# All pairs of the second MLP matrix by seven products, with sums kept in PSUM over the slices and two of the seven added by VectorE

## Chip, cores and metric

One NeuronCore of a Trainium2 chip runs the whole kernel. The metric is the device time of one execution in microseconds. Engines are called as in the profile: PE (TensorE) multiplies, PEld loads its stationary operand, DVE (VectorE) and ACT (ScalarE) do elementwise work, POOL (GpSimd) next to nothing here, and SP issues the DMAs.

## What is computed

A decoder trunk of two layers over 256 tokens with a model dimension of 2048, all in float32. Layer 0 mixes with a gated short convolution, layer 1 with latent attention (16 heads); each layer then has an MLP, and each sub-layer ends in a post-norm `x <- LN(alpha*x + f(x))`. The change lies in the two MLPs:

```python
def sq_relu_mlp(x, w1, w2):                       # x (256, 2048), w1 (2048, 8192), w2 (8192, 2048)
    return jnp.square(jax.nn.relu(x @ w1)) @ w2

h = layer_norm(ALPHA * h + mix, ln_g[layer, 0], ln_b[layer, 0])
h = layer_norm(ALPHA * h + sq_relu_mlp(h, mlp_w1[layer], mlp_w2[layer]), ln_g[layer, 1], ln_b[layer, 1])
```

## The kernel before, in words

**Precision.** Every float32 operand is split into a high part that PE multiplies in one pass and a low rest: ACT makes the high part by a cast (`split`, L127), DVE the rest by a subtraction (L128). A product then takes three matmuls: high x high, high x low, low x high (`dot`, L300, L302, L303).

**Weights.** They stream from DRAM in loads of 128 x 1024 (512 KB) on SP's queue into a ring of `RAW` = 5 raw buffers, are split, and stand in a ring of `WA` = 8 pairs of high and low buffers. `take` (L183) hands the next weights to the consumer and, before that, writes out the preparing steps up to `LOOK` = 5 steps ahead, so the order in which DVE and ACT get their work follows the order of consumption; a scheduler then moves single instructions within it.

**An MLP** (`mlp`, L575) goes over the hidden dimension in eight slices, q = 0 to 7, of eight chunks of 128 each. In the up half of a slice, `products` (L288) makes eight sums over 16 blocks of w1, each a matmul of 512 columns and one of 256 (L215, L219); `hidden` (L713) takes each out of PSUM, applies relu and square, and splits it. In the down half the slice is multiplied with its rows of w2 and added to the output, which is kept in SBUF as `acc`, 256 tokens x 2048 columns.

**The six inner slices** (`FAST`, q = 1 to 6, in both layers twelve) form the down products two by two: a pair of hidden chunks and the two halves of the tokens make a 2 x 2 block matrix, the pair's weights for two blocks of 512 columns another, and seven products in place of eight give the four results (`FACTORS`, L339). The price are sums of the blocks: of the inputs by `form` (L703), four DVE operations and a split for each pair; of the weights in `prepare` (L141), three DVE subtractions (L162, L166, L169) and two further splits for each pair. There are two groups g of two column blocks and four pairs j in each. `MIXED` = "sssp" says that in the first group only three pairs go that way ("s"); the fourth ("p") is done plainly with eight products, from two plain loads of w2. So a slice has three fast pairs and a plain one, then four fast pairs.

**Sums.** The seven running sums of a group are not folded into the output at each slice. Four of them ("1", "5", "7", "6": `OWN`) have a place of their own in the tile `sums`, three have the place of an output block. Before a group's matmuls ACT copies a sum from its place into a PSUM bank (`resumed`, L608), the matmuls add onto it, and afterwards ACT copies it back (`put_back`, L615) or DVE adds a freshly begun sum onto the place (`keep`, L618). All seven leave PSUM after each group. `fold` (L669) combines them in the last slice. Of the eight banks, four serve the up sums, and they change places with the others from slice to slice.

**Order around it.** The residual `xres` (16 chunks of 128 x 256) stays in SBUF throughout. In layer 0, `begin` subtracts a mean from its chunks in the last slice; in layer 1, `extra` turns it by 32 transposes on PE and adds it to `acc`, a quarter in each of the slices 1 to 4.

Of the kernel before, what the change touches and what calls it, by code (L numbers as in the profile page):

```python
# [16 lines left out]
P = 128  # L17
W = 256 + 2
T = 256
# [14 lines left out]
RAW, WA = 5, 8  # L34
# [3 lines left out]
MIXED = "sssp"  # L38
EVEN = (QC - 1, "22")
# [7 lines left out]
WO_G = 3  # L47
BEHIND = (2, 2, 2, 3, 2, 2, 3)
# [5 lines left out]
def trunk(ctx: ExitStack, tc: tile.TileContext, xT, vecs, lead, w_first, w_in, w_out, w_kv, w_q, w_uk, w_uv,  # L54
# [12 lines left out]
    xres = act.tile([P, NC, T], F32, tag="xres", name="xres")  # L67
    for tag, columns in (("c", 4096), ("a2", 4128), ("a1", 4128), ("b", 8256)):
        act.tile([P, columns], F32, tag=tag, name=f"at_{tag}")
# [7 lines left out]

    stream = []
# [20 lines left out]
    stream += halves(w_o) + mlp_stream(1)  # L99

# [40 lines left out]
    def prepare(i):  # L141
# [7 lines left out]
        r1, r2 = (load_raw(f"{i}_{j}", src) for j, src in enumerate(stream[i]))  # L149
        out = []  # L150

        def finished(r, name):
# [3 lines left out]

        b22, (b21, b12) = r1[:, BW:], (r2[:, :BW], r2[:, BW:])
# [12 lines left out]
        f = state["fast"].tile([P, 2, BW], F32R, tag="t4", name=f"t4_{i}", bufs=2)  # L170
        split(f[:, 0, :], f[:, 1, :], t4)
        b1, t13, b2 = ([[v.rearrange("p b c -> p (b c)")[:, o:o + BW] for v in w] for o in (0, BW)] for w in out)
        ready[i] = {"11": b1[0], "22": b1[1], "21": b2[0], "T2": b2[1], "T1": t13[0], "T3": t13[1],
                    "T4": [f[:, 0, :], f[:, 1, :]]}
# [168 lines left out]
    def fast_products(ps, x, forms, j, fresh, ready, onto=()):  # L343

        b, = take(1)
        a = {"11": held(x[2 * j], 0), "12": held(x[2 * j + 1], 0), "22": held(x[2 * j + 1], 1)}
        for i in range(4):
            a[f"S{i + 1}"] = [forms[:, j, o, i * P:(i + 1) * P] for o in range(2)]
        for p, l, r in FACTORS:
            dot(ps[p], b[r], a[l], p in fresh, p in ready, onto=p in onto)  # L350

# [40 lines left out]
    class Norm:  # L392
# [10 lines left out]
        def prepare(self, m, bank=None):  # L403

            d = xres[:, m, :]
# [11 lines left out]
        def count(self, m):  # L417
            d = xres[:, m, :]
# [21 lines left out]
        def wide(self, m):  # L440
            d, x, g = xres[:, m, :], self.xd[m], self.gain(m)[0]
# [31 lines left out]
        def normal(self, m, dst=None):  # L473

            g, b = self.gain(m)
            d = xres[:, m, :]
# [22 lines left out]
    def add(ps, m):  # L499
        d = xres[:, m, :]  # L500
        nc.vector.tensor_tensor(d, d, ps[:, :T], ALU.add)

    def summed(ln, pss, add, m0=0):

        for m, ps in enumerate(pss, m0):
            add(ps, m)
# [40 lines left out]
    ln = Norm(0, ALPHA)  # L547
    for m in range(NC):
# [19 lines left out]
        if m >= NC // 2:  # L568
            for k in range(2 * m - NC, 2 * m - NC + 2):
                ln.prepare(k)  # L570
    nc.sync.dma_start(id_t, ident)
    ln.widen("a1", "a2")
    summed(ln, chain(products(1, z), lagged(NC - 1, z)), residual)

    def mlp(idx, ln, blocks, fast, begin=None, extra=None, last=False):  # L575
# [25 lines left out]
        sums = fast.tile([P, 4, 2, BW], F32, name=f"sums{idx}")  # L601

        def place(p, g):

            return sums[:, OWN.index(p), g, :] if p in OWN else \
                block(*{"2": (2 * g, 0), "3": (2 * g + 1, 0), "4": (2 * g, 1), "22": (2 * g + 1, 1)}[p])

        def resumed(p, g, name, bank):  # L608

            ps = psum(name, bank)  # L610
            if q != FAST[0] or p not in OWN:
# [3 lines left out]
        def put_back(p, g, ps):  # L615
            nc.scalar.copy(place(p, g), ps)

        def keep(p, g, ps):  # L618

            at = place(p, g)  # L620
            if q == FAST[0] and p in OWN:
# [4 lines left out]
        def resume(busy, free, ps, m):  # L626

            b2, b3, b4, b6 = free
            b1, b5, b7, b22 = busy
# [558 lines left out]
```

## Time and profile before

| what | us |
|---|---|
| three timed runs | 1996.66, 1998.59, 1999.63; median 1998.59 |
| span of the profiled execution (the page gives no other time for it) | 1994.9 |
| PE busy | 1987.7 |
| PEld busy | 1737.2 |
| DVE busy | 1709.4 |
| ACT busy | 1354.9 |

The granted TensorE clock is 1.000. HBM is read at 381.78 MB in all, 192 GB/s over the span. How to read it: matmuls are pipelined, so the duration of one (some 390 ns for 512 columns) is longer than the distance between two starts; busy time is the union over an engine's instructions. The inner slices of layer 0 begin near 454, 537, 620, 703, 787 and 870 us, those of layer 1 near 1396, 1480, 1564, 1648, 1732 and 1815 us; the up half takes a little over half of each.

### The profile page before, as it was taken

The page shows a single profiled execution, that of the slowest core. Times are in us where ns is not written, and L with a number is a line of the kernel's source. Part 1 is how long each engine was busy: PE and PEld are TensorE (multiplying, and loading weights), DVE is VectorE, ACT ScalarE, POOL GpSimd, SP SyncE. Part 2 cuts the span into 40 slices and gives each one's busy share as a digit, 9 for nine tenths or more (in the row PEclk, how much of TensorE's full clock was granted, in tenths as well). Part 3 has the DMA queues.
Part 4 walks back from the last instruction along what each step waited for, and adds up shares of the span by engine and source line. Part 5 has one row for each costly group of instructions (what it writes and reads, how often), then busy time and mean ns, then how long its engine had stood idle before and what let it go on. Part 6 is the DMA issues. An engine that isn't in the chain of part 4 may idle for free.

```text
span 1994.9 us, 30180 instructions
## 1 busy us (share of the span) xinstructions
PE 1987.7 (100%) x11110; PEld 1737.2 (87%) x11110; DVE 1709.4 (86%) x2555; ACT 1354.9 (68%) x2154; POOL 2.3 (0%) x21
## 2 busy tenths in 40 slices
PE   9999999999999999999999999999999999999998
PEld 8888888988888888888889998898888888888886
DVE  8667667797999989989978988777899999999985
ACT  6444445586778778777756755558677787887772
POOL 0000000000000000000000000000000000000000
PEclk9999999999999999999999999999999999999999
DMA  8666666565657466574855543656464656656483
GB/s 318 205 191 187 190 190 190 179 193 157 212 170 251 148 216 221 177 243 147 281 171 159 170 140 123 201 180 195 146 233 155 232 161 220 222 178 233 150 269 130
DMA packets 106853, 385.85 MB, mean 193 GB/s; under 512 B 11857, under 2 KB 12625, under 8 KB 106449
## 3 DMA queue, kind: packets, MB, share of 16 engines
q1 hardware_dynamic: 106560, 383.79, 59.5%
q8 instruction: 87, 1.43, 0.3%
q14 instruction: 62, 0.50, 0.1%
q10 hardware_dynamic: 144, 0.13, 0.0%
HBM read 381.78 MB, written 2.10 MB: 192 GB/s over the span
## 4 chain that ended last, share of the span: by engine, by line
PE 98%; DVE 1%; ACT 1%; issue 0%; DVEq 0%; ACTq 0%
PE ps_u L215 20%; PE ps_l L215 13%; PE ps_u L219 10%; PE ps_l L219 7%; PE ps_f L300 4%; PE ps_f L303 4%; PE ps_f L302 4%; PE ps_r L303 4%; PE ps_r L302 4%; PE ps_r L300 4%; PE ps_d L300 2%; PE ps_d L302 2%; PE ps_d L303 2%; PE ps_w L249 2%; PE ps_w L248 2%; PE ps_w L247 2%
## 5 line engine op out<-in xcount | busy, mean ns | idle before, releaser
L128 DVE TENSOR_TENSOR lo<-raw,hi 128x1024 fp32r<-128x1024 f32 x710 | 861.8, 1220 | 190.6 <-ACT hi L127 119.9
L127 ACT CAST hi<-raw 128x1024 fp32r<-128x1024 f32 x710 | 741.8, 1051 | 247.4 <-PE ps_l L215 98.1
L215 PE MATMUL ps_u<-xhl,hi 128*128 128x512 f32 x1792 | 621.7, 392 | 0.0
L219 PE MATMUL ps_u<-xhl,lo 128*128 128x256 f32 x1792 | 498.2, 279 | 0.0
L215 PEld LDWEIGHTS ps_u<-xhl,hi 128*128 128x128 f32 x1792 | 334.5, 187 | 73.6 <-ACT acc L595 0.2
L219 PEld LDWEIGHTS ps_u<-xhl,lo 128*128 128x128 f32 x1792 | 338.1, 189 | 1.8
L215 PE MATMUL ps_l<-xhl_a,hi 128*128 128x512 f32 x704 | 244.1, 393 | 0.0
L219 PE MATMUL ps_l<-xhl_a,lo 128*128 128x256 f32 x704 | 195.4, 279 | 0.0
L215 PEld LDWEIGHTS ps_l<-xhl_a,hi 128*128 128x128 f32 x704 | 132.1, 188 | 29.9
L219 PEld LDWEIGHTS ps_l<-xhl_a,lo 128*128 128x128 f32 x704 | 131.9, 188 | 0.2
L127 ACT CAST hi_t<-raw_t 128x1024 fp32r<-128x1024 f32 x84 | 88.5, 1054 | 45.8 <-DVE raw_t L162 41.4
L162 DVE TENSOR_TENSOR raw_t<-raw,raw 128x1024 f32<-128x1024 f32 x84 | 102.3, 1218 | 1.8 <-DMA raw<-in_w2f_dram 1.5
L128 DVE TENSOR_TENSOR lo_t<-raw_t,hi_t 128x1024 fp32r<-128x1024 f32 x84 | 102.4, 1219 | 0.2
L718 ACT ACTIVATE fp<-fp 128x256 f32<-128x256 f32 x96 | 40.0, 416 | 63.2 <-DVE fp L356 62.6
L215 PE MATMUL ps_l<-z,hi 128*128 128x512 f32 x240 | 82.4, 391 | 0.0
L300 PE MATMUL ps_d<-hi,h 128*128 128x512 f32 x192 | 75.0, 391 | 0.0
L302 PE MATMUL ps_d<-lo,h 128*128 128x512 f32 x192 | 75.0, 390 | 0.0
L303 PE MATMUL ps_d<-hi,h 128*128 128x512 f32 x192 | 74.8, 389 | 0.0
L249 PE MATMUL ps_w<-xd,hi 128*128 128x258 f32 x256 | 72.7, 284 | 0.0
L248 PE MATMUL ps_w<-xd,lo 128*128 128x258 f32 x256 | 72.3, 282 | 0.0
L247 PE MATMUL ps_w<-xd,hi 128*128 128x258 f32 x256 | 72.3, 282 | 0.0
L215 PE MATMUL ps_l<-oT,hi 128*128 128x512 f32 x208 | 71.3, 391 | 0.0
(296 smaller groups left out, 3963.7 us busy)
## 6 DMA issues: line engine op xcount, KB each, us to landing
raw<-in_w_dram SPq DMA_DIRECT2D x344, 512.0 KB, 4.5
raw<-in_w2f_dram SPq DMA_DIRECT2D x168, 512.0 KB, 3.9
raw<-in_w_in_dram SPq DMA_DIRECT2D x88, 512.0 KB, 4.2
raw<-in_w_out_dram SPq DMA_DIRECT2D x32, 512.0 KB, 3.7
raw<-in_w_o_dram SPq DMA_DIRECT2D x32, 512.0 KB, 4.2
raw<-in_w_kv_dram SPq DMA_DIRECT2D x10, 512.0 KB, 3.7
raw<-in_w_q_dram SPq DMA_DIRECT2D x8, 512.0 KB, 4.0
raw<-in_w_uk_dram SPq DMA_DIRECT2D x8, 512.0 KB, 3.9
```

The source lines that it names most:

```text
L127: nc.scalar.copy(hi, src)
L128: nc.vector.tensor_tensor(lo, src, hi.bitcast(F32), ALU.subtract)
L162: nc.vector.tensor_tensor(t.rearrange(two, a=2), b12.unsqueeze(1).to_broadcast([P, 2, BW]), r1.rearrange(two, a=2), ALU.subtract)
L215: nc.tensor.matmul(ps, w[blk // 8][0][:, blk % 8, :], x, start=first, stop=False)
L219: nc.tensor.matmul(ps[:, :T], w[blk // 8][1][:, blk % 8, :], x[:, :T], start=False, stop=last)
L247: nc.tensor.matmul(ps[:, :W], hi, x[k][:, :W], start=k == 0, stop=False)
L248: nc.tensor.matmul(ps[:, :W], lo, x[k][:, :W], start=False, stop=False)
L249: nc.tensor.matmul(ps[:, :W], hi, x[k][:, W:], start=False, stop=k == NC - 1)
L300: nc.tensor.matmul(ps, x[0], w[0], start=first, stop=False, skip_group_check=onto)
L302: nc.tensor.matmul(ps[:, at], x[0], w[1][:, at], start=False, stop=False, skip_group_check=onto)
L303: nc.tensor.matmul(ps, x[1], w[0], start=False, stop=last, skip_group_check=onto)
L718: nc.scalar.activation(f, f, AF.Relu)
```

## The change

- Every pair of both groups is a fast one; `MIXED` and the plain pairs go.
- The two groups change their order from slice to slice (`groups`): the second group of a slice is the first of the next. Four of its sums ("3", "1", "5", "7") stay in their PSUM banks over the next up half; "2", "6" and "4" are copied out and, in the middle of the next up half, in again (`first_sums`).
- At the change of group inside a slice the last pair of the first group is followed product by product: as soon as a sum's last matmul is issued, it is taken out (`turn`) and its bank takes the next sum of the second group. Sums "3" and "1" (`FRESH`) begin there from nothing, and DVE adds them onto their place when they leave; the other five are copied in and out by ACT.
- The input factors of a pair lie in one tile of seven blocks, made by three DVE operations and one split (`form`); relu and square run over the two chunks of a pair at once.
- The residual is written to DRAM (`parked`) in slice 1 of layer 0, the tile `sums` takes its place in SBUF, and in slice 7 it is loaded again (`xback`). `begin` moves from the last slice to slice 1. In layer 1 all of `extra` moves to slice 1.
- The rings grow: `RAW` from 5 to 7, `WA` from 8 to 9.
- A way of preparing weight factors ahead and storing them in DRAM (`EARLY`) is written but empty here; its code is left out below.

```diff
-RAW, WA = 5, 8
+RAW, WA = 7, 9
-MIXED = "sssp"
-EVEN = (QC - 1, "22")
+EARLY = {}
+FRESH = ("3","1")
...
+    def groups(q):
+        return (1, 0) if (q - FAST[0]) % 2 == 0 else (0, 1)
...
-            for j, kind in enumerate(MIXED):
-                out += [(w2f[l, q, 1, j, 0], w2f[l, q, 1, j, 1])] if kind == "s" else \
-                    halves(w2[l, q, 2, j]) + halves(w2[l, q, 3, j])
-            out += [(w2f[l, q, 0, j, 0], w2f[l, q, 0, j, 1]) for j in range(QC // 2)]
+            for i, g in enumerate(groups(q)):
+                for j in range(QC // 2):
+                    out.append((w2f[l, q, g, j, 0], w2f[l, q, g, j, 1]) + made.get((l, q, i, j), ()))
...
+        def first_sums(ps, banks, m):
+            g = groups(q)[0]
+            for p in {3: ("3", "1", "5", "7") if q == FAST[0] else (), 4: "2", 5: "6", 6: "4"}.get(m, ()):
+                banks.setdefault(p, busy[m % 4])
+                ps[p] = begun_sum(p, g, f"ps_r{p}", banks[p])
+
+        def new_sum(p):
+            return p in FRESH or (q == FAST[0] and p in OWN)
+
+        def begun_sum(p, g, name, bank):
             ps = psum(name, bank)
-            if q != FAST[0] or p not in OWN:
+            if not new_sum(p):
                 nc.scalar.copy(ps, place(p, g))
             return ps
...
+        def keep(p, g, ps, since):
             at = place(p, g)
-            if q == FAST[0] and p in OWN:
+            if p not in FRESH or (since == FAST[0] and p in OWN):
                 nc.scalar.copy(at, ps)
             else:
                 nc.vector.tensor_tensor(at, at, ps, ALU.add)
...
+            def begin_next(p, bank):
+                after[p], place_of[p] = begun_sum(p, second, f"ps_f{p}", bank), bank
+
+            def turn(p):
+                keep(p, first, ps[p], max(q - 1, FAST[0]) if p in order[:4] else q)
+                i = order.index(p) + 1
+                if i < len(order):
+                    begin_next(order[i], banks[p])
+
+            def end(p):
+                if p not in stay:
+                    keep(p, second, after[p], q)
+
+            held_on = set(order[:4]) if q > FAST[0] else set()
+            for j in range(n):
+                if j == n - 1:
+                    begin_next(order[0], spare)
+                fast_products(ps, h, j, new - held_on if j == 0 else (), ps if j == n - 1 else (),
+                              set(ps) - (new - held_on), turn if j == n - 1 else None)
+            for j in range(n):
+                fast_products(after, h, j, new if j == 0 else (), after if j == n - 1 else (),
+                              set(order) - new, end if j == n - 1 else None)
...
+            def form(j, u):
+                a21, a11, a12, s1, s2, s4 = (u[:, i * P:(i + 1) * P] for i in (0, 1, 3, 4, 6, 7))
+                two = u.rearrange("p (i c) -> p i c", c=P)
+                nc.vector.tensor_tensor(s1, a21, u[:, 2 * P:3 * P], ALU.add)
+                nc.vector.tensor_tensor(two[:, 5:7, :], two[:, 0:5:4, :], a11.unsqueeze(1).to_broadcast([P, 2, P]),
+                                        ALU.subtract)
                 nc.vector.tensor_tensor(s4, a12, s2, ALU.subtract)
-                split(forms[:, j, 0, :], forms[:, j, 1, :], sf.rearrange("p i c -> p (i c)"))
+                f = factors[j // 2][:, j % 2]
+                split(f[:, 0, :], f[:, 1, :], u[:, P:])
...
-                    if extra and m == 0 and q <= NB:
+                    if extra and q == FAST[0] and m < NB:
                         for t in range(2):
-                            extra(block, q - 1, t, busy[2 + t])
+                            extra(block, m, t, busy[2 + t])
+                    if begin and q == FAST[0]:
+                        begin(range(max(2 * m, 1), 2 * m + 2))
+                        nc.sync.dma_start(parked[:, 2 * m:2 * m + 2, :], held_x[0][:, 2 * m:2 * m + 2, :])
+                    if q == FAST[0] and m == QC - 1:
+                        sums = act.tile([P, 4, 2, BW], F32, tag="xres", name=f"sums{idx}")
...
+                if begin and q == NQ - 1:
+                    held_x[0] = act.tile([P, NC, T], F32, tag="xres", name="xback")
+                    for k in range(0, NC, 4):
+                        nc.sync.dma_start(held_x[0][:, k:k + 4, :], parked[:, k:k + 4, :])
```

More of the change, by code (lines that the diff above doesn't have):

```diff
@@ L47 @@
 WO_G = 3
+MAKE_FROM = 6
 BEHIND = (2, 2, 2, 3, 2, 2, 3)
@@ L169, in prepare @@
         nc.vector.tensor_tensor(t4, b21, b12, ALU.subtract)
[L170 to L174, printed above, removed]
+        ready[i] = {**named((("11", "22"), ("T1", "T3"), ("21", "T2"))), "T4": fourth(t4)}
         yield
```

193 lines of the change are left out of this document (102 added, 91 removed).

## The prediction

> **What bounds the kernel now.** Read the page first: the busy shares, then the chain that ended last.
>
> ```profile
> span 1994.9 us, 30180 instructions
> ...
> PE 1987.7 (100%) x11110; PEld 1737.2 (87%) x11110; DVE 1709.4 (86%) x2555; ACT 1354.9 (68%) x2154; POOL 2.3 (0%) x21
> ...
> PE 98%; DVE 1%; ACT 1%; issue 0%; DVEq 0%; ACTq 0%
> ```
>
> TensorE is the chain: whoever takes matmuls away shortens the kernel, as long as the engines that feed it keep up. VectorE's mean of 86% hides stages. So the second view is the windows, one for each slice of the hidden dimension that is multiplied with the seven-product scheme (here three inner ones of the first layer, two of the second, one down half, and the ends).
>
> ```profile
> 536.98:620.21 83.23, 83.23 (x429) 71.28 (x429) 78.12 (x102) 66.78 (x104) 0.00 (x0) 1.00 0.61 199
> 620.21:703.43 83.22, 83.22 (x429) 71.27 (x429) 80.15 (x104) 66.50 (x102) 0.00 (x0) 1.00 0.63 206
> 869.88:954.04 84.16, 83.70 (x430) 71.13 (x429) 79.04 (x103) 66.35 (x103) 0.00 (x0) 1.00 0.59 199
> 954.04:1037.00 82.96, 82.96 (x433) 70.94 (x433) 68.07 (x93) 51.83 (x84) 0.53 (x1) 1.00 0.72 234
> 1563.72:1647.81 84.09, 84.09 (x437) 71.86 (x437) 79.71 (x105) 66.81 (x102) 0.00 (x0) 1.00 0.61 197
> 1815.13:1898.36 83.23, 83.23 (x429) 71.28 (x429) 78.53 (x103) 66.20 (x102) 0.00 (x0) 1.00 0.59 200
> 1898.36:1994.90 96.54, 90.84 (x451) 75.52 (x450) 67.46 (x91) 45.81 (x75) 0.00 (x0) 1.00 0.56 196
> ```
>
> ```profile
> 581.50:620.21 38.71, 38.71 (x174) 32.12 (x174) 38.54 (x46) 32.12 (x47) 0.00 (x0) 1.00 0.59 187
> ```
>
> The columns are the stretch, its length, and the busy time of PE, PEld, DVE, ACT. A slice takes 83.23 us with TensorE never idle, and VectorE is busy for 78 to 80 of them, about 79.2: it has 4.0 us to spare. In the down half it has 0.2 us. In one slice (869.88) TensorE already stood still, for 84.16 - 83.70 = 0.46 us. The waits of that stretch say on what:
>
> ```profile
> DVE lo L128 <- ACT hi L127: 5.3, 9, 1.4
> ...
> ACT hi L127 <- DMA raw<-in_w_dram: 3.9, 5, 1.3
> ...
> PE ps_f L300 <- ACT acc L616: 0.5, 1, 0.5
> ```
>
> A sum had not been copied out of its bank in time. **So TensorE bounds, and VectorE is the close second in the twelve slices that the change touches.** The rest of TensorE's 7.2 us of idle time is the start and the last window (96.54 - 90.84); the change reaches neither.
>
> **Part 1: matmuls removed.** A plain pair cost 8 products of 3 matmuls, one of them split in two (25), a fast pair costs 21. The built program has 48 matmuls fewer: in each slice 2 of 512 columns and 2 of 256.
>
> ```profile
> L300 PE MATMUL ps_r<-hi,h 128*128 128x512 f32 x168 | 65.5, 390 | 0.0
> ...
> L302 PE MATMUL ps_r<-lo,h 128*128 128x512 f32 x156 | 60.7, 389 | 0.0
> ...
> L302 PE MATMUL ps_r<-lo,h 128*128 128x256 f32 x24 | 4.7, 280 | 0.0
> ```
>
> ```profile
> 868.23 0.39 PE L300 MATMUL ps_f<-t,h 128*128 128x512 f32 x1
> ...
> 868.91 0.39 PE L215 MATMUL ps_u<-xhl,hi 128*128 128x512 f32 x1
> 869.14 0.28 PE L219 MATMUL ps_u<-xhl,lo 128*128 128x256 f32 x1
> 869.25 0.40 PE L215 MATMUL ps_u<-xhl,hi 128*128 128x512 f32 x1
> ```
>
> The 390 ns are latency; what counts is the pitch: three of 512 columns in 868.91 - 868.23 = 0.68 us, 0.227 each; one of 256 in 0.11. A slice saves 2 x 0.227 + 2 x 0.115 = 0.69 us, twelve **8.3 us**, to a slice of 82.54. [...]
>
> **Part 2: VectorE's work.** The added fast pair needs, for weights, one more subtraction of 1024 columns, two of 512, and two more splits.
>
> ```profile
> L128 DVE TENSOR_TENSOR lo_t<-raw_t,hi_t 128x1024 fp32r<-128x1024 f32 x84 | 102.4, 1219 | 0.2
> L162 DVE TENSOR_TENSOR raw_t<-raw,raw 128x1024 f32<-128x1024 f32 x84 | 102.3, 1218 | 1.8 <-DMA raw<-in_w2f_dram 1.5 <-DVE lo L128 0.3
> L169 DVE TENSOR_TENSOR raw<-raw 128x512 f32<-128x512 f32 x84 | 57.8, 688 | 1.3
> ...
> L128 DVE TENSOR_TENSOR t<-raw,t 128x512 fp32r<-128x512 f32 x84 | 57.4, 683 | 0.0
> L356 DVE TENSOR_TENSOR fp<-ps_u,t 128x256 f32<-128x256 f32 x96 | 40.1, 418 | 0.0
> L128 DVE TENSOR_TENSOR forms<-sf,forms 128x512 fp32r<-128x512 f32 x48 | 32.9, 685 | 0.1
> ...
> L624 DVE TENSOR_TENSOR acc<-acc,ps_f 128x512 f32<-128x512 f32 x24 | 16.3, 680 | 0.1
> ...
> L709 DVE TENSOR_TENSOR sf<-sf,fp 128x128 f32<-128x128 f32 x48 | 13.9, 289 | 0.9
> ```
>
> ```profile
> 849.77 1.22 DVE L128 TENSOR_TENSOR lo_t<-raw_t,hi_t 128x1024 fp32r<-128x1024 f32 x1
> 850.91 0.68 DVE L169 TENSOR_TENSOR raw<-raw 128x512 f32<-128x512 f32 x1
> 851.51 1.22 DVE L162 TENSOR_TENSOR raw_t<-raw,raw 128x1024 f32<-128x1024 f32 x1
> ```
>
> The pitch is 1.14 us for 1024 columns and 0.60 for 512 (the second view), so the pair adds 2 x 1.14 + 3 x 0.60 = 4.08 us a slice. The two plain loads that go were split too, and the fast pair's two are, so these cancel. The input factors get cheaper: four sums of 128 columns and two splits of 512 become two of 128, one of 256 and one split of 896, which no row shows; between 512 and 1024 columns in proportion it is 1.0 us. That saves 0.36 us a pair, 1.4 a slice. The adds of sums onto SBUF fall from 34 to 24 (the ten sums<-sums adds stay), 0.5 us a slice. Net **+2.1 us a slice**: VectorE needs 79.2 + 2.1 = 81.3 of the 82.54 us. Its spare time falls from 4.0 to 1.2 us.
>
> **Part 3: what of that reaches TensorE.** VectorE's idle time lies in the first part of a slice; of the last 60 us of the slice that begins at 786.66 it is busy for all but 0.8:
>
> ```profile
> 810.00:869.88 59.88, 59.88 (x296) 50.74 (x295) 59.06 (x78) 47.34 (x73) 0.00 (x0) 1.00 0.52 160
> ```
>
> How near it comes there is seen in the last fast pair: its last factor against the matmul that reads it (least and greatest margin of the twelve slices).
>
> ```profile
> 950.46 0.68 DVE L128 TENSOR_TENSOR t<-raw,t 128x512 fp32r<-128x512 f32 x1
> ...
> 1474.51 0.68 DVE L128 TENSOR_TENSOR t<-raw,t 128x512 fp32r<-128x512 f32 x1
> ```
>
> ```profile
> 952.61 0.39 PE L302 MATMUL ps_f<-t,h 128*128 128x512 f32 x1
> ...
> 1478.20 0.39 PE L302 MATMUL ps_f<-t,h 128*128 128x512 f32 x1
> ```
>
> 952.61 - 951.14 = 1.5 us and 1478.20 - 1475.19 = 3.0. The change takes 4.08 + 0.69 from it, and 1.2 for the two adds of the fresh sums, which now stand between the groups; the cheaper input factors give back 0.8 in this stretch. From 1.5 to 3.0 it falls by 5.2 to -3.7 to -2.2, unless VectorE begins further ahead. It can: nine factor buffers for eight and seven load buffers for five let it prepare one split and one subtraction more, 2 x 1.14 = 2.3 us, and possibly a third, 3.4. That leaves -1.4 to +1.2. The idle time says how much lead is to be had: 3.9 us of ScalarE's waits in the slice quoted were for loads, which two more buffers should mostly cover, while hand-overs between VectorE and ScalarE remain (VectorE waited nine times for ScalarE there, 0.6 us each). I take 1.5 us of idle time that VectorE can't avoid against 1.2 that it has: **0.3 us of stall a slice, 3.6 in all**. Bounds: none, and (all of today's 4.0) 2.8 a slice.
>
> **Part 4: the rest.** ScalarE loses some 84 bank copies of about 0.5 us and half its small activations, and gains twelve splits: from 66.5 to about 63 us a slice; that is hidden beside TensorE, except at the change of group. There the fifth product's bank follows a chain, seven copies out and in, one split and two copies more:
>
> ```profile
> 929.87 1.54 ACT L616 COPY sums<-ps_r 128x512 f32<-128x512 f32 x3
> ```
>
> At 0.5 us a copy and 1.0 a split that is 5.1 us, and TensorE's order leaves 24 matmuls, 5.4 us: hidden, by 0.3. For the add of sum "3" VectorE has 23 matmuls, 5.2 us, less its own 0.7. The 0.46 us stall of today is of the kind that goes or stays with these; I count it as gone. The residual: 2 MB out during the first fast slice, where the matmuls begin after a light stage, and 2 MB in behind the eleventh of sixteen loads of the last slice (954.04: the DMA engines at 0.72 with 234 GB/s, so 512 KB take some 1.6 us, and four 6.5), with two blocks of down sums, over 20 us, before it is read. Nothing; 6.5 us at most if loads queue behind it. The sixteen subtractions of the residual's mean moved with it lie before the first fast slice in the built order. In the second layer the 32 transposes of the residual now fall into one slice and share two banks with its matmuls; the order fills the gaps with other matmuls; I take 0.5 us, between none and 3.
>
> **Sum.** -8.3 - 0.5 + 3.6 + 0.5 = -4.7 us: the profiled execution goes from 1994.9 to 1990.2, and the median, 3.7 above that span, from 1998.6 to **1994**.
>
> **The rivals.** *Full cover* (0.15): the deeper rings give the whole 3.4 us of lead and no slice waits: 1998.6 - 8.8 = 1989.8. For it: the waits for loads are of the kind that more buffers cover. Against it: the margins above. *The hand-over at the group change* (0.2): ScalarE's chain has 0.3 us to spare, and is itself behind a split that waits for VectorE; if it misses by as much as in 869.88, 0.46, on top of the 0.3, the sum is 1989.8 + 12 x 0.76 = 1998.9, no change. *VectorE as the bound* (0.24): the two adds wait for TensorE at the head of VectorE's queue, and behind them stand the factors of the next pairs; with forced idle time above 1.2 + 0.69 = 1.9 us a slice it is slower than before. At 3.0 us, as 620.21 has in all, each slice is 1.8 longer than 82.54 and the time 1989.8 + 21.6 = 2011. [...] That the change does not do what it says is excluded by the built program's 48 matmuls.
>
> **How the numbers follow.** The forecast (0.41) spans stalls of 0.1 to 0.6 us a slice, 1991 to 1997.5. Two runs can't be told apart within 0.2%, 4 us: below 1994.6 is faster. Faster: full cover and somewhat over half of the forecast, 0.40; same: the rest and the hand-over, 0.36; slower: 0.24. The range, 1989.5 to 2007, takes in full cover, forecast, hand-over and the mild end of VectorE's case.
>
> **What would show it.** Windows of the slices: TensorE at 82.5 us busy, of a length near 82.8; VectorE at 81 or more. The stalls as waits of ps_f matmuls for VectorE's lo and t, or for the adds of "3" and "1". Idle time of VectorE that stays near 3 us while TensorE waits would prove the third rival; waits for ScalarE's copies alone, the second. I am wrong at the root if VectorE's busy time is not near 81.

## The result and the profile after

The changed kernel takes 2017.57 us (median of 4 runs, 2016.94 to 2018.47), the kernel before beside it 1998.57 (4 runs, 1996.66 to 1999.63): ratio 1.0094, with a 95% interval of 1.008 to 1.0109. It is slower by 0.9%, where 1994 was forecast and 2007 was the upper end of the range.

The page of the changed kernel, the lines that answer to those of before:

```profile
span 2016.7 us, 29855 instructions
...
PE 2003.2 (99%) x11062; PEld 1728.1 (86%) x11062; DVE 1738.7 (86%) x2509; ACT 1310.8 (65%) x1950; POOL 2.3 (0%) x21
...
PE 86%; DVE 10%; ACT 3%; issue 2%; DMA 0%; DVEq 0%; ACTq 0%; SPq 0%
```

The 48 matmuls are gone (11110 to 11062 records), and so are 204 instructions of ScalarE. But TensorE's share of the chain fell from 98% to 86%, and VectorE's rose from 1% to 10%. TensorE's 99% busy must not mislead: the end of a matmul is modelled, and some that come late are drawn longer (0.45 and 0.50 us for 0.39 in the first timeline below). So I count from start to start, by windows of whole slices (the first slice, two inner ones and the last of the first layer, an inner one of the second; then one inner slice by halves):

```profile
453.56:540.63 87.07, 84.43 (x426) 71.73 (x424) 74.09 (x91) 54.89 (x76) 0.00 (x0) 0.98 0.51 151
625.32:709.99 84.67, 84.39 (x426) 70.18 (x424) 81.58 (x99) 62.51 (x85) 0.00 (x0) 1.00 0.61 199
709.99:794.65 84.66, 84.39 (x425) 70.25 (x424) 81.51 (x99) 62.50 (x85) 0.00 (x0) 1.00 0.60 199
879.33:962.16 82.83, 82.56 (x419) 68.85 (x417) 80.10 (x98) 60.76 (x83) 0.00 (x0) 1.00 0.60 198
1664.37:1749.03 84.66, 84.40 (x426) 70.18 (x424) 81.50 (x99) 62.70 (x85) 0.00 (x0) 1.00 0.59 199
```

```profile
709.99:755.31 45.32, 45.32 (x257) 39.14 (x256) 42.98 (x54) 33.69 (x46) 0.00 (x0) 1.00 0.65 232
755.31:794.65 39.34, 39.07 (x170) 31.11 (x169) 38.53 (x46) 28.81 (x39) 0.00 (x0) 1.00 0.53 161
```

Seven of the ten inner slices are 84.65 to 84.70 us long, where 82.54 was TensorE's own need and 83.23 the length before; the second slice of the second layer takes 85.54. In a slice of 84.66 VectorE is busy for 81.5 us and idle for 3.1. (The last slice of each layer looks like 82.83, since seven of its matmuls, 1.6 us, are drawn behind the first matmul of the next.) Stage by stage, in us:

| stretch | before | after | more |
|---|---|---|---|
| up to the first fast slice | 452.8 | 453.6 | 0.8 |
| six fast slices, first layer | 500.3 | 508.6 | 8.3 |
| up to the second layer's | 441.5 | 445.2 | 3.7 |
| six fast slices, second layer | 502.8 | 509.2 | 6.4 |
| the rest | 97.5 | 100.1 | 2.6 |

Of the 3.7 and the 2.6, 1.6 each are those seven matmuls. Three things make up the loss.

**Stops at the end of a down half.** The timeline of TensorE there (start, duration; in brackets the idle time and its releaser):

```profile
792.47 0.45 PE L350 MATMUL ps_f<-t,h_4a 128*128 128x512 f32 x1
793.16 0.50 PE L352 MATMUL ps_f<-lo,h_4a 128*128 128x512 f32 x1 [0.24 <-DVE lo L160]
793.50 0.39 PE L353 MATMUL ps_f<-hi,h_4a 128*128 128x512 f32 x1
```

0.69 us lie between two starts that are 0.227 apart when nothing is late, and 0.34 between the next two: the last pair's `lo` and `hi` come late from VectorE and ScalarE. In all the down half takes 39.34 us for 168 x 0.227 = 38.1: stops of 1.2 us. In the second slice of each layer it takes 40.3, with stops of some 2 us.

**A longer pitch in the up half.** It takes 45.32 us for 128 pairs of a 512 and a 256 column matmul, with no gap of its own. In the second and in the fourth slice:

```profile
571.50 0.39 PE L265 MATMUL ps_u<-xhl,hi 128*128 128x512 f32 x1
571.73 0.28 PE L269 MATMUL ps_u<-xhl,lo 128*128 128x256 f32 x1
571.85 0.39 PE L265 MATMUL ps_u<-xhl,hi 128*128 128x512 f32 x1
572.08 0.28 PE L269 MATMUL ps_u<-xhl,lo 128*128 128x256 f32 x1
572.19 0.39 PE L265 MATMUL ps_u<-xhl,hi 128*128 128x512 f32 x1
```

```profile
731.29 0.40 PE L265 MATMUL ps_u<-xhl,hi 128*128 128x512 f32 x1
731.53 0.28 PE L269 MATMUL ps_u<-xhl,lo 128*128 128x256 f32 x1
731.64 0.40 PE L265 MATMUL ps_u<-xhl,hi 128*128 128x512 f32 x1
731.87 0.28 PE L269 MATMUL ps_u<-xhl,lo 128*128 128x256 f32 x1
731.99 0.40 PE L265 MATMUL ps_u<-xhl,hi 128*128 128x512 f32 x1
```

Two pairs take 0.69 us in the one and 0.70 in the other; over whole up halves the mean is 347 ns a pair and 353, at a granted clock of 1.00 both times. 347 is what every up half of the kernel before has. From the third slice on (the second in the second layer) the changed kernel has 353: 128 x 6.5 ns = 0.8 us in each of eleven up halves. The two second slices show the price: their down halves are the same 40.3 us, and the one with 347 ns is 84.69 us long, the one with 353 ns 85.54.

**One long stop.** In the first slice of the first layer, at the change of group, TensorE stands for 2.64 us, and the granted clock (the column before the last two) drops behind it:

```profile
520.51 0.50 PE L350 MATMUL ps_f<-hi,h_1c 128*128 128x512 f32 x1 [2.64 <-DVE acc L691]
```

```profile
519.00:521.00 2.00, 0.49 (x2) 0.45 (x3) 2.00 (x3) 1.94 (x4) 0.00 (x0) 1.00 0.61 127
521.00:523.00 2.00, 2.00 (x9) 1.53 (x8) 1.96 (x4) 2.00 (x4) 0.00 (x0) 0.71 0.34 137
523.00:525.00 2.00, 2.00 (x6) 1.62 (x5) 2.00 (x3) 1.36 (x2) 0.00 (x0) 0.50 0.52 139
525.00:527.00 2.00, 2.00 (x9) 1.60 (x9) 2.00 (x2) 0.00 (x0) 0.00 (x0) 0.93 0.81 205
```

2 x (0.29 + 0.50 + 0.07) = 1.7 us of clock are lost, so it stood at one half for 3.4 us: this stop costs 2.6 + 1.7. In the second layer the first slice has none; its 86.84 us hold the 32 transposes of the residual, which took 0.86 us in each of four slices before (84.09 for 83.23) and now fall into one.

So, over 82.54: most inner slices are longer by 1.2 us of stops and 0.8 of pitch, the second ones by 2.0 of stops and, in the second layer, 0.8 of pitch, and the first slice of the first layer by 4.5.

### The profile page after: what moved, and what is told of

Its sections match the earlier page's. It is cut to its first block, busy times and chain, and to the rows that moved or that the text cites. A ratio compares the mean times of both kernels' runs of the same rounds, so it can differ in the third digit from the quotient of the medians.

```text
span 2016.7 us, 29855 instructions
## 1 busy us (share of the span) xinstructions
PE 2003.2 (99%) x11062; PEld 1728.1 (86%) x11062; DVE 1738.7 (86%) x2509; ACT 1310.8 (65%) x1950; POOL 2.3 (0%) x21
## 4 chain that ended last, share of the span: by engine, by line
PE 86%; DVE 10%; ACT 3%; issue 2%; DMA 0%; DVEq 0%; ACTq 0%; SPq 0%
PE ps_u L265 20%; PE ps_l L265 13%; PE ps_u L269 10%; PE ps_l L269 7%; DVE lo L160 3%; PE ps_f L352 3%; PE ps_f L353 3%; PE ps_f L350 2%; DVE lo_t L160 2%; PE ps_d L350 2%; PE ps_d L353 2%; PE ps_d L352 2%; PE ps_w L299 2%; PE ps_w L298 2%; PE ps_w L297 2%
## 5 line engine op out<-in xcount | busy, mean ns | idle before, releaser
L265 PE MATMUL ps_u<-xhl,hi 128*128 128x512 f32 x1792 | 631.9, 397 | 0.5 <-ACT hi L159 0.4
L159 ACT CAST hi_t<-raw_t 128x1024 fp32r<-128x1024 f32 x96 | 100.9, 1051 | 72.1 <-DVE raw_t L216 47.4
L216 DVE TENSOR_TENSOR raw_t<-raw,raw 128x1024 f32<-128x1024 f32 x96 | 116.9, 1218 | 7.3 <-DMA raw<-in_w2f_dram 6.6
L160 DVE TENSOR_TENSOR lo_t<-raw_t,hi_t 128x1024 fp32r<-128x1024 f32 x96 | 117.0, 1219 | 6.0 <-ACT hi_t L159 5.1
L159 ACT CAST t<-raw 128x512 fp32r<-128x512 f32 x96 | 59.3, 618 | 16.3 <-PE ps_r L353 12.0
```

What stands on the lines that cost most here:

```text
L159: nc.scalar.copy(hi, src)
L160: nc.vector.tensor_tensor(lo, src, hi.bitcast(F32), ALU.subtract)
L216: nc.vector.tensor_tensor(t.rearrange(two, a=2), b12.unsqueeze(1).to_broadcast([P, 2, BW]), r1.rearrange(two, a=2), ALU.subtract)
L265: nc.tensor.matmul(ps, w[blk // 8][0][:, blk % 8, :], x, start=first, stop=False)
```

## The experiments

Theory A, by now: VectorE works in order (the sum whose add TensorE waited for in the first slice had its last matmul at 512.73 us, of 0.39, and VectorE began the add at 519.77, behind seven instructions begun after the sum was there), an inner slice takes its 81.5 us of work plus the idle time that it can't avoid, and that idle time lies where the rings are full. The waits of the changed kernel from 715 to 740 us, where most of it falls, say so (total, times, longest):

```profile
ACT hi L159 <- PE ps_u L265: 3.9, 4, 1.8
ACT hi_t L159 <- PE ps_u L265: 1.5, 1, 1.5
DVE lo L160 <- ACT hi L159: 1.3, 4, 0.6
```

ScalarE waits for TensorE to give factor buffers back, and VectorE for ScalarE: I read this as both being as far ahead as nine buffers let them, and not far enough for the down half. VectorE is idle for 2.0 of its 3.1 us in these 25 us. Rival B is the hand-over of the banks at the change of group.

### Rings undone

```diff
-RAW, WA = 7, 9
+RAW, WA = 5, 8
```

> The changed kernel with the rings of before, 5 load buffers and 8 factor buffers for 7 and 9. Theory A (VectorE sets the pace in order, and it can run ahead only as far as the factor buffers go: in a slice from 710 us of the changed kernel it is busy for 81.5 of 84.66 us and idle for 3.1, while ScalarE waits for TensorE to free factors): one factor buffer less is one split of 1.14 us less of lead, so the idle time grows to 4.3 us, the inner slices to 85.8 us and the time by about 12 x 1.1 to 2031. Rival B (the hand-over of the banks at the change of group holds TensorE up): the rings don't matter, 2017.6. Rival C (the rings were no help, the added work alone costs it): 2017.6 as well, with VectorE's idle time still 3.1 us.

### Five load buffers, ten factor buffers

```diff
-RAW, WA = 7, 9
+RAW, WA = 5, 10
```

> The changed kernel with 5 load buffers and 10 factor buffers, in the same space. Theory A: one split more of lead, idle time of VectorE 3.1 to 2.0 us, inner slices 83.5 and the time about 2004; if the longer pitch in the up half (353 ns for a pair of matmuls of 512 and 256 columns from the third slice on, 347 in the kernel before) goes away with the stops, 1994. Rival B: 2017.6. Rival D (the loads, not the factors, limit the lead): 5 load buffers make it slower than 2017.6.

Measured 2046.6 us (ratio 1.0246, 1.023 to 1.0261) and 2029.39 (1.0159, 1.0144 to 1.0174). An inner slice of each:

```profile
800.11:887.34 87.23, 85.35 (x426) 70.09 (x424) 82.00 (x99) 62.71 (x85) 0.00 (x0) 1.00 0.56 193
```

```profile
793.14:879.41 86.27, 84.30 (x425) 70.04 (x424) 81.62 (x99) 62.73 (x85) 0.00 (x0) 1.00 0.57 195
```

VectorE's work is nearly that of the changed kernel; its idle time is 5.2 and 4.7 us. So the rings move it, as theory A says, and B and C fall. That the change brought deeper rings kept it from being 2.5% slower. But theory A's sizes were wrong, 2031 and 2004 for 2046.6 and 2029.39: the loads limit the lead too, as rival D has it. With five load buffers ScalarE waits 4.2 us for loads in the second slice shown, with seven 0.6 us in the one from 709.99. Two factor buffers (5, 8 to 5, 10) are worth 17 us, and from 5, 10 to 7, 9 two load buffers outweigh one factor buffer by another 12. If each factor buffer is worth some 9 us, a load buffer is by these numbers worth about 10, an estimate: neither ring alone is the limit.

### Less work for VectorE

```diff
-        nc.vector.tensor_tensor(t4, b21, b12, ALU.subtract)
```

> The changed kernel without the subtraction that makes the fourth factor (512 columns, eight in a slice), so VectorE has 8 x 0.60 = 4.8 us less in a slice; the fourth factor is then taken from the loaded values as they are. Theory A: VectorE needs 76.7 us of a slice, no slice waits, TensorE's own 82.5 us remain. If the pitch of 353 ns in the up half follows from the stops, it goes back to 347 and the time is about 2017.6 - 12 x 2.2 - 3 = 1988; if it belongs to the program, slices of 83.3 us and about 1998. Rival B: the stop at the change of group stays, over 2012.

This kernel leaves out arithmetic, so it shows where the time goes and is no way to get it. Measured 1991.3 us (0.9969, 0.9957 to 0.998).

```profile
701.78:784.32 82.54, 82.54 (x426) 70.58 (x424) 76.73 (x90) 62.61 (x86) 0.00 (x0) 1.00 0.60 207
```

Theory A holds in the inner slices: with 76.7 us of work none waits, the length is the 82.54 of part 1, and the pitch is 347 ns in all up halves but for stretches of the second layer's first, among the transposes. So the changed order of the matmuls, with the same buffers, allows the short pitch. The change of group, with all its adds and copies, stops nothing in an inner slice: B falls again. One thing is mixed in: without the subtraction ScalarE's split of the fourth factor no longer waits for VectorE either. The next but one experiment, which only adds work, and the stored factors below answer for the work alone. The whole change is worth 6 us then and not 8.3, since the first slices keep 1.2 (83.72 for 82.54) and, beside the transposes, 0.7 us.

### All sums copied; one sum fresh

```diff
-FRESH = ("3","1")
+FRESH = ()
```

> The changed kernel with no sum begun fresh at the change of group: all seven are copied in and out by ScalarE. VectorE has two adds of 0.60 us less in a slice, ScalarE four copies of 0.5 us more. Theory A: idle time of VectorE unchanged at 3.1 us, work 80.3, inner slices 83.4 and the time about 2003, or 1993 if the pitch goes back to 347 ns. Rival B (the hand-over): ScalarE's chain at the change of group is four copies, 2 us, longer, slices of 85 us and more, 2025.

```diff
-FRESH = ("3","1")
+FRESH = ("3",)
```

> The changed kernel with one sum begun fresh (the first product's) in place of two: VectorE one add of 0.60 us less, ScalarE two copies of 0.5 us more. With two the inner slices are 84.67 us (work 81.5, idle 3.1), with none 85.42 (80.6, 4.8). Theory A with ScalarE's copies as a part of the idle time: between the two, 85.0 us and 2018 to 2020. If the long stop in the first slice comes of the first product's add, it stays.

Measured 2020.21 us (1.0113, 1.0097 to 1.0128) and 2016.68 (1.0094, 1.0079 to 1.0109). For none fresh, an inner slice and its waits:

```profile
791.73:877.15 85.42, 84.46 (x425) 70.36 (x424) 80.61 (x97) 64.28 (x89) 0.00 (x0) 1.00 0.58 198
```

```profile
DVE lo L160 <- ACT hi L159: 2.9, 7, 0.9
...
DVE fp L408 <- ACT t L407: 1.2, 1, 1.2
PEld ps_f L350 <- ACT hi_t L159: 1.2, 1, 1.2
```

Theory A failed here as I had put it: work fell to 80.6 us, but the idle time rose to 4.8. Idle time isn't a constant. I put the rise down to the four copies, which stand between ScalarE's splits: VectorE waits for ScalarE for 4.3 us in this slice, for 2.6 in the changed kernel's from 709.99. That fits, but no run separates it. The fresh sums pay for themselves in the inner slices: 0.9 us more work for 1.7 less idle time. With one fresh sum the time is that of two, below what I expected: an inner slice takes 84.65 us, with 80.8 of work and 3.8 of idle time. Its first slice still has the stop, of 1.7 us for 2.6, and without loss of clock (84.51 us).

### More work for VectorE in the kernel before

```diff
-        nc.vector.tensor_tensor(t4, b21, b12, ALU.subtract)
+        for _ in range(2 if count % 7 in (0, 2, 4, 6) else 1):
+            nc.vector.tensor_tensor(t4, b21, b12, ALU.subtract)
```

> The kernel before, with the subtraction of the fourth factor done twice in four of the seven fast pairs of a slice: 4 x 0.60 = 2.4 us more of VectorE's work in a slice and nothing else. Theory A (VectorE's work and the idle time that it can't avoid are what a slice needs): 79.2 + 2.4 = 81.6 us of work, and with the rings of 5 and 8 at least 3.1 us of idle time, slices of 84.7 us or longer for 83.2, so 2016 to 2030. Rival B (the regrouping of the sums, not the work, made the change slow): no change, 1998.6.

Measured 2015.8 us (1.0083, 1.0068 to 1.0098).

```profile
792.36:877.40 85.04, 84.40 (x429) 71.18 (x428) 81.33 (x107) 66.53 (x103) 0.00 (x0) 1.00 0.57 198
```

With the old grouping, the old rings and the plain pair, 2.4 us more of VectorE's work bring slices of 85.0 us and the changed kernel's time within 2 us. The added work alone is enough to bring stops and a time like that: theory A. It does not show that the new arrangement is free. With the same rings of 5 and 8 the changed kernel's slice above is 87.2 us with 5.2 of idle time, here it is 85.0 with 3.7; what of the difference is the regrouping and what the eighth fast pair's third load buffer, no run separates.

### Two of eight subtractions left out

```diff
-        nc.vector.tensor_tensor(t4, b21, b12, ALU.subtract)
+        if count % 4:
+            nc.vector.tensor_tensor(t4, b21, b12, ALU.subtract)
```

> The changed kernel with the subtraction of the fourth factor left out in two of the eight pairs of a slice, 1.2 us less for VectorE; the fourth factor of those pairs is taken from the loaded values as they are. Theory A, with the idle time of 3.1 us constant: 80.3 + 3.1 = 83.4 us an inner slice, with the longer pitch gone where the stops go: 2003, 1996 with the pitch. If the idle time isn't constant but grows as the work shrinks, as it did when the sums weren't begun fresh, slices stay at 84.7 and the time near 2017.

Measured 2001.76 us (1.0015, 1.0005 to 1.0024), near the 2003 of theory A. The inner slices are 83.4 us in the mean, but of two kinds. A slice of each layer:

```profile
623.30:706.06 82.76, 82.76 (x425) 70.53 (x424) 79.52 (x97) 62.10 (x85) 0.00 (x0) 1.00 0.60 203
1651.81:1735.94 84.13, 83.89 (x426) 70.42 (x424) 79.93 (x97) 62.59 (x85) 0.00 (x0) 1.00 0.58 202
```

Most of the first layer's run at 82.8 us and 347 ns, the second layer's middle ones at 84.13 and 353, with a stop of 0.4 us at each end. So the same program has two ways to run near the bound, and agreement with 83.4 is in part luck. A slice mostly runs as the one before it, not always: the fifth of the first layer has 353 ns between two with 347, with nothing but a matmul 0.03 us late at its start. Why, these runs don't tell.

### Does a stop bring the long pitch?

```diff
-        nc.vector.tensor_tensor(t4, b21, b12, ALU.subtract)
+        for _ in range({13: 7, 27: 7, 62: 9}.get(count, 1)):
+            nc.vector.tensor_tensor(t4, b21, b12, ALU.subtract)
```

> The kernel before, with the fourth factor's subtraction repeated in the last fast pair of three slices only: 6 times more in the second and the fourth slice of the first layer (3.6 us), 8 times more in the third of the second layer (4.8 us). With margins of 1.5 to 3.0 us TensorE stops for 1 to 3 us three times. If a stop shortly before an up half leaves TensorE in the longer pitch (353 ns for a pair of 512 and 256 columns for 347), the up halves behind the three stops show it, until something sets it back, 0.8 us a slice: 1998.6 + 5 + up to 7 = 2004 to 2011. If the pitch belongs to the changed program and not to stops, all up halves stay at 347 ns and the time is the stops alone, 2002 to 2005.

Measured 2005.43 us (1.0036, 1.0021 to 1.005). The late matmuls of the last product (`ps_f`) have moved into the next up half, so the stops stand 8 to 12 us behind its first matmul. The first of the three:

```profile
626.72 0.28 PE L221 MATMUL ps_u<-xhl,lo 128*128 128x256 f32 x1
626.84 0.39 PE L217 MATMUL ps_u<-xhl,hi 128*128 128x512 f32 x1
629.38 0.50 PE L302 MATMUL ps_f<-t,h 128*128 128x512 f32 x1 [2.15 <-ACT t L127]
```

Ahead of it the pairs of this up half run at 347 ns, in the rest of it at 353, and in the next one at 347 again. Behind the second stop, of 0.7 us, it is 353, then 347; behind the third, of 1.5, it is 347. Three stops were few, so:

```diff
-        for _ in range({13: 7, 27: 7, 62: 9}.get(count, 1)):
+        for _ in range(7 if count % 7 == 6 else 1):
```

> The kernel before, with the fourth factor's subtraction repeated six times more in the last fast pair of every fast slice: twelve stops of 0.7 to 2.2 us just before an up half, in a program with the matmuls of before. If the pitch of 353 ns in an up half is what such a stop leaves behind more often than not (two of three so far), seven to nine of the twelve up halves show it and the time is 1998.6 + 12 x 1.4 + 8 x 0.8 = 2022. If the two were chance, at most three show it, and 2017.

Measured 2021.51 us (1.0119, 1.0098 to 1.0141). Twelve stops of 1.0 to 1.6 us stand 8 to 10 us into up halves. In seven of these the rest runs at 353 ns (in one only from some 6 us behind the stop, where a matmul comes 0.2 us late), in five at 347. One of the five had 353 ahead of the stop: the short pitch can come back at a stop too. The first up half of the second layer has 353 without any stop. With the earlier run it is nine of fifteen, in a program that without them has 347 in every up half. That a stop can bring the long pitch is shown, since it changes there within an up half; nine of fifteen is no firm rate, and what decides it each time is open.

What it costs is seen once more where two neighbours differ in nothing else, as in the run of the next section (up half and down half of the fourth slice, then of the third):

```profile
706.34:750.86 44.52, 44.52 (x258) 39.05 (x256) 42.62 (x54) 33.70 (x46) 0.00 (x0) 1.00 0.65 236
750.86:790.19 39.33, 39.06 (x171) 31.07 (x169) 38.70 (x46) 28.81 (x39) 0.00 (x0) 1.00 0.54 162
621.71:667.03 45.32, 45.32 (x257) 39.15 (x256) 42.81 (x54) 33.76 (x46) 0.00 (x0) 1.00 0.65 230
667.03:706.34 39.31, 39.04 (x170) 31.13 (x169) 38.52 (x46) 28.81 (x39) 0.00 (x0) 1.00 0.52 162
```

The down half is the same, the up half 0.80 us longer, and VectorE spends that idle: with the short pitch its idle time is 2.5 us, with the long one 3.3.

### The residual's stores on another queue

```diff
-                        nc.sync.dma_start(parked[:, 2 * m:2 * m + 2, :], held_x[0][:, 2 * m:2 * m + 2, :])
+                        nc.gpsimd.dma_start(parked[:, 2 * m:2 * m + 2, :], held_x[0][:, 2 * m:2 * m + 2, :])
```

> The changed kernel with the eight stores of the residual issued from GpSimd's queue in place of SyncE's. In the first slice of the first layer VectorE waited 5.7 us for loads of combined weights, TensorE stopped for 2.8 us at the change of group and ran at half its clock for 3.4 us: 87.1 us for 84.7. If the stores ahead of the loads cause that, the first slice takes 83 to 84.7 us and the time is 2014. If they don't, 2017.6.

Measured 2015.71 us (1.0089, 1.0074 to 1.0104). The first slice takes 82.75 us, without a stop:

```profile
453.33:536.08 82.75, 82.75 (x426) 70.40 (x424) 72.91 (x90) 55.48 (x76) 0.00 (x0) 1.00 0.48 153
```

The waits ahead of the change of group, first in the changed kernel, then here:

```profile
DVE raw_t L216 <- DMA raw<-in_w2f_dram: 5.7, 4, 2.2
```

```profile
DVE raw_t L216 <- DMA raw<-in_w2f_dram: 2.3, 3, 1.0
```

So the stores on SyncE's queue bring the long stop, by way of the loads behind them: VectorE, held up by the loads, came late with the add that TensorE then waited for. They need the other rings for it, though: with 5 and 10 buffers and the stores where they were the first slice takes 82.56 us. The second slice is 85.6 us long here, with 353 ns in its up half, behind no more than a lateness of 0.1 us at the seam; two other up halves have 347 in return. In the profiled executions the span falls by 4.4 us, as much as the first slice gained; the medians differ by 1.9, and no other execution has a trace to say why.

### The order of the preparations

```diff
-LOOK = 5
+LOOK = 6
```

> The changed kernel with each preparation written one step earlier in the order (6 steps ahead of its use for 5). Theory A with the rings as the limit of the lead: no change, 2016 to 2019, VectorE's idle time still about 3 us in an inner slice. If the written order limits the lead, the idle time falls by about one split, 1.1 us, and the time to 2005.

Measured 2012.68 us (1.0067, 1.0054 to 1.0081): less than I expected of full rings, far from the other end.

```profile
706.69:791.18 84.49, 84.23 (x426) 70.36 (x424) 81.42 (x99) 62.64 (x85) 0.00 (x0) 1.00 0.59 199
```

This inner slice is 0.2 us shorter and VectorE's idle time 3.1 as before: the written order isn't what limits the lead. The rest of the 5 us is a first slice of 84.17 us and three up halves of the second layer at 347 ns.

### Relief with the arithmetic kept

GpSimd does nothing in the fast slices, so it was given the subtraction:

```diff
-        nc.vector.tensor_tensor(t4, b21, b12, ALU.subtract)
+        nc.gpsimd.tensor_tensor(t4, b21, b12, ALU.subtract)
```

> The changed kernel with the fourth factor's subtraction (512 columns, eight in a slice) on GpSimd in place of VectorE: 4.8 us less for VectorE in a slice, as in the run without it (1991.3). Theory A: if GpSimd takes about as long as VectorE (0.7 us), the same 1991 to 1993. Rival: GpSimd is several times slower, or slows VectorE while it runs; the split behind the subtraction then comes late, and the slices are as long as now or longer, 2017 and above.

Measured 2065.76 us (1.0332, 1.0317 to 1.0348).

```profile
721.59:810.52 88.93, 84.74 (x425) 71.61 (x424) 83.87 (x91) 63.00 (x85) 14.43 (x8) 0.98 0.56 192
```

GpSimd takes 14.43 / 8 = 1.8 us for what takes VectorE 0.69, and VectorE is busy for 83.9 us with 76.7 us of work left to it, so it is slowed too: in the third to sixth slices its subtraction `raw_t` of two SBUF operands takes 1445 ns in the mean for 1217 in the changed kernel, its add with a PSUM operand 674 for 677. GpSimd takes 2.6 times as long here. Why the one of VectorE's operations is slowed beside it and the other isn't, no run shows.

The other way is the kernel's own: factors made ahead, where VectorE has time, and stored.

```diff
-EARLY = {}
+EARLY = {0: ((1, 3),), 1: ((1, 3),)}
...
-            if k != l:
-                continue
...
-    before_mlp = making(0, making_in.enter_context(tc.tile_pool(name="making0", bufs=2)))
+    before_mlp = making(0, making_in.enter_context(tc.tile_pool(name="making0", bufs=1)))
```

> The changed kernel with the combined factors of one pair in each of the twelve slices (the last of the second group) made during the first layer's convolution, where VectorE has time, stored in DRAM and loaded again: VectorE has 1.14 + 2 x 0.60 = 2.3 us less in a slice. Theory A: 81.5 - 2.3 + 3.1 of idle time = 82.3 us, below TensorE's 82.5: no stops in the inner slices, pitch 347 ns, about 2017.6 - 12 x 2.1 = 1992, with the one long stop in the first slice still there. Rival: the stops are elsewhere and only move, 2005 to 2017.

Measured 2035.41 us (1.0181, 1.0165 to 1.0196). The slices did what theory A says:

```profile
740.34:823.10 82.76, 82.76 (x426) 70.58 (x424) 79.09 (x96) 62.72 (x85) 0.00 (x0) 1.00 0.61 212
```

But the first one began at 490.3 us for 453.6: in the convolution VectorE stood in front of these loads, for 39.8 us in all. The making has one set of buffers here, in this run and the two that follow, so each load also waits for the stores before it (25.0 us of SyncE's queue between 140 and 240 us in the last of the three); more sets were not tried. Two attempts to make that cheaper, first by spreading the steps:

```diff
-MAKE_FROM = 6
+MAKE_FROM = 0
...
             nc.gpsimd.dma_start(to24, r1)
+            yield
...
-            if m % 3 == 0:
+            if m % 2 == 0:
```

> The changed kernel with stored factors for one pair in each slice, as in the run before (inner slices of 82.8 us there, but 37 us lost in the convolution, where VectorE stood in order behind loads that GpSimd's queue had issued late), with the making now begun with the first chunk of the convolution and its loads issued one step later than the stores and one ahead of the work. Theory A: the slices stay at 82.8 us and the convolution loses nothing: 2035.4 - 37 = 1998, to 1995. If a wait of VectorE for these loads stays, over 2005.

Measured 2037.92 us (1.0201, 1.0186 to 1.0216): no better, the first slice begins at 493.6. Then with the loads, and the residual's stores, exchanged between the queues:

```diff
-                nc.gpsimd.dma_start(r, src)
+                nc.sync.dma_start(r, src)
...
-                        nc.sync.dma_start(parked[:, 2 * m:2 * m + 2, :], held_x[0][:, 2 * m:2 * m + 2, :])
+                        nc.gpsimd.dma_start(parked[:, 2 * m:2 * m + 2, :], held_x[0][:, 2 * m:2 * m + 2, :])
```

> The changed kernel with stored factors for one pair in each slice, their sources now loaded by SyncE's queue and not by GpSimd's, and with the residual's stores on GpSimd's queue. If the making costs nothing beside TensorE, the slices of 82.65 to 82.8 us of the two runs with stored factors and a first slice of about 83 instead of 85.7 give 1993 to 1997, a little below the kernel before. If VectorE still stands behind loads or stores of the making in the convolution, over 2005, and then the loads' queue was not the reason.

Measured 2004.13 us (1.0023, 1.0013 to 1.0033). Over the run before, the other queue for the loads gained 30 us of the 40; 10 remain. Two waits of VectorE in the convolution, and TensorE behind the second:

```profile
209.87 1.23 DVE L124 TENSOR_TENSOR m<-m,m 128x1024 f32<-128x1024 f32 x1 [5.17 <-DMA m<-in_w2f_dram]
225.44 1.23 DVE L124 TENSOR_TENSOR m<-m,m 128x1024 f32<-128x1024 f32 x1 [4.74 <-DMA m<-in_w2f_dram]
228.57 0.58 PE L268 MATMUL ps_l<-xhl_a,lo 128*128 128x256 f32 x1 [4.10 <-DVE lo L159]
```

VectorE still stands in front of a load, 5.2 and 4.7 us, with TensorE's weights behind it. From the first fast slice to the end this kernel takes 2003.1 - 463.7 = 1539.4 us, the kernel before 1994.9 - 452.8 = 1542.1: the fewer matmuls are worth 2.7 us here, less than the relief costs. None of these versions that keeps the arithmetic beats the kernel before.

## Why the prediction was wrong

- **What bounded the kernel before, and part 1: right.** 48 matmuls fewer, 82.54 us a slice; the run with less work for VectorE gives 82.54.
- **Part 2: right.** VectorE's work was forecast at 81.3 us and measured at 81.5 (the adds of sums fell to 22, not 24).
- **Part 3: here it failed**, at "I take 1.5 us of idle time that VectorE can't avoid against 1.2 that it has". It can't avoid 2.5 with TensorE's short pitch, and has 3.1 in the kernel as it runs. I had read the idle time of one slice as waits for loads that two more buffers would mostly cover. They do cover those: ScalarE's waits for loads fell from 3.9 us in the slice quoted to 0.6 in the one from 709.99, and its longest waits there are for TensorE and VectorE. But the run of 5 and 8 buffers shows that this kernel needs the deeper rings to come down from 5.2 us to 3.1; they don't bring it from 4.0 to 1.5. So the stops are 1.2 to 2.0 us a slice for the 0.3 forecast. The third rival had the right engine and a price near the right one: "at 3.0 us ... each slice is 1.8 longer", measured 2.1. That closeness is in part luck, since 0.8 of the 2.1 is pitch, which it didn't have. Nor are its two adds at the head of VectorE's queue what does it in the inner slices: without them the idle time is 4.8 us and the slice 85.4, and with both, but less work, nothing stops. Only the long stop of the first slice waits for such an add.
- **A term that I didn't have:** the pitch of the up half, 0.8 us in eleven up halves, some 9 of the 21.8 us. Nothing in the trace of before showed that a stop outlasts itself.
- **Part 4.** ScalarE's chain at the change of group held in the inner slices, so the second rival is out as the cause there; its margin was thinner than written, since nine copies at 0.5 us and a split are 5.5 us, not 5.1, beside TensorE's 5.4. The stall of 0.46 us went as I said. "Nothing" for the residual's stores was wrong: they brought the one stop of 2.6 us and 1.7 us of lost clock. I had looked at the bandwidth (0.72 busy, in the slice of the loads back) and not at what stands behind them in SyncE's queue at that place. For the transposes I took 0.5 us; they cost what they cost before, now in one slice, and 0.7 to 0.9 more in that first slice.
- **The sum:** from 1990.2 forecast to 2016.7 are 26.5 us: some 11 of stops (0.7 to 1.9 more than forecast in each of ten slices), 9 of pitch in the eleven up halves, 4 for the one long stop. Of the remaining 2 or so, 1.3 lie in the output projection, whose pairs (about 200) take 353 ns as well, for 347 before; they do so in the run without stops in the inner slices too, so a stop there isn't the only thing that brings the long pitch.
- **The chance:** 0.24 for VectorE as the bound was, I think, too little, with 98% of the slice filled in my own sum and an idle time of 4.0 us that no row showed to be free.

## What to carry over

When an engine's work comes to within a few per cent of the stage, take the whole idle time that it has today as unavoidable unless a row shows otherwise, and price the stage as work plus that idle time: here 81.3 + 4.0 = 85.3 us, against 84.7 measured and 82.8 forecast. It is a first price and no constant; the slices shown above have 2.5 to 5.2 us beside 80.6 to 82.0 us of work. Ask what limits its lead (which ring is full, and who gives the buffer back) before counting on deeper rings. And a stop of the bounding engine can cost more than its own length, as the one of 2.64 us did here, with 1.7 us of clock lost behind it.

## What the runs showed of the hardware

- A pair of matmuls of 512 and 256 columns runs at 347 or at 353 ns in the mean, at the same granted clock, over long stretches. Stops of 0.7 to 2.15 us inside an up half left 353 behind them in nine of fifteen cases, and the pitch also changed without a stop. Down halves, of 512 columns alone, show 0.227 us a matmul where nothing is late.
- A stop of 2.64 us was followed by 3.4 us at half TensorE's clock; those of 1.7 us (one sum fresh) and 2.15 us (three stops) above were not. The length doesn't decide it: in the second run with stored factors a stop of 1.81 us in the convolution was followed by half the clock, and in the first such run one of 2.15 us was, and one of 3.46 us wasn't. What decides it, these runs don't show.
- GpSimd slows VectorE beside it: what took 76.7 us in the run without the subtraction took 83.9 in the run with it on GpSimd, which was busy for 14.4 us of the slice.
- A matmul of split operands is one record in the trace; a plain float32 one is two. In the kernel before, 32 matmuls of the attention scores (L945) left 64 records, and with 256 columns the next begins 0.43 us behind such a pair's start, for 0.12 with split operands.

The stop of 1.81 us, and the half clock behind it (0.50, the column before the last two):

```profile
163.33 0.39 PE L268 MATMUL ps_l<-xhl_a,lo 128*128 128x256 f32 x1 [1.81 <-DVE lo L159]
```

```profile
165.00:167.00 2.00, 2.00 (x7) 1.70 (x7) 1.97 (x5) 0.00 (x0) 1.07 (x2) 0.50 0.90 313
```
